# Last attention head: TensorE's steps in a fixed order between half sums of the output projection

## The chip, the cores and the metric

The kernel runs on one core of a Trainium2 chip. The metric is the device time of one execution in microseconds, from the first to the last instruction and what lies around them; the median of several runs stands for a kernel. TensorE's clock is 2.4 GHz, or 1.2 GHz where it is throttled.

## The reference

The model is a trunk of two residual layers on a sequence of 1024 tokens of width 1024, in float32, with a norm at the end. The change lies in the first layer. It has two branches on one normed input: an SSD scan (Mamba-2, 1024 channels), and a differential attention with 8 heads. An attention head has two query and two key maps of width 64 and one value of width 128:

```python
s = einsum(q, k) * scale + bias[rel]          # two maps, causal
p = softmax(s)
w = p[:, :, 0] - lam * p[:, :, 1]
o = rmsnorm(einsum(w, v), subln_w) * (1 - lam_init)
y_b = o * silu(g)
h = x + concat([y_a, y_b]) @ w_out            # w_out: 2048 x 1024
```

The second layer (a gated linear recurrence) has the same kind of output projection, `out_proj`.

## The kernel before

Matmuls of the projections run in split float32: an operand is a high part and a rest, and a product is three matmuls (high by high, high by rest, rest by high). One group of 12 such matmuls of 512 columns (four blocks of 128 in the inner dimension, three products each) adds four input blocks of one token block into one PSUM bank. I call it a half sum: two of them (`kq` 0 and 1) make a sum over 8 blocks of 128, which is all of one branch.

**The attention of one head** is `att_core` (from line 592). A head has 8 query blocks of 128 tokens, block `i` sees `i + 1` key blocks. `soft(i)` issues the scores of both maps on TensorE (line 613, into the PSUM tag `big`, two buffers), on DVE the bias and the maximum (lines 617 and 621), on ACT the exponential with its sum (line 627), on DVE the reciprocals (631 to 633) and the weighted difference of the two maps (line 634). `values(i)` transposes the difference on TensorE (line 645, into `s1`), copies it to SBUF on ACT (line 647) and multiplies it with the values (line 649). In the trace such a matmul of 128 columns in plain float32 counts as two. After four blocks `norm` scales, squares and sums on ACT (657, 660), takes the power on GpSimd (line 150) and multiplies on DVE (663); a `tail` later transposes the result (668), gates it on DVE (695) and stores it to HBM (696). Block `i + 1`'s scores are traced ahead of block `i`'s transposes.

**The output projection** is `out_proj` (from line 716). Its early part reads the SSD branch: 16 tiles `u`, split on ACT and DVE (lines 709 and 710), weights in two column halves `n`, and for each half 16 half sums, whose sums DVE adds to the input rows (line 767). That is 32 half sums, 384 matmuls at line 187. The late part does the same with the attention's output, which it reads back from HBM (lines 706, 712, 713), and ends in the next layer's norm.

**What sets the order.** The framework's scheduler decides the order of each engine's instructions from a time model. Code under `manual_schedule(engines={PE})` is the exception: there TensorE's instructions stand in the order in which the code issues them. Before the change only the SSD branch stood under it (line 902). `layer0` traces the heads one after the other, then `out_proj`, and the scheduler puts the early half sums into the heads' gaps where their inputs are there. The inputs come when the last projection that reads the layer's normed input is over: the projection of head 7 (line 176), which the scheduler puts beside head 5. So heads 6 and 7 have the early half sums beside them: the 16 of the first column half beside the first six blocks of head 6, the 16 of the second half from there on through head 7.

Of the kernel before, what the change touches and what calls it, by code (L numbers as in the profile page):

```python
# [70 lines left out]
def run(pieces):  # L71
    for _ in pieces:
        pass
# [515 lines left out]
    out += [(qs[m], (ks[m], xs[m])) for m in range(2)]  # L589


def att_core(S, h, qk, V, sg, yb, tail):

    nc = S.nc
    hh = h % 2
    near = S.t("ph" if h % 2 else "cm", [P, 256])

    for i in range(8):
        o = 127 - 16 * i
        nc.sync.dma_start(near[16 * i:16 * i + 16],  # L600
                          S.tz_d[h, o:o + 16 * 383].rearrange("(p w) -> p w", w=383)[:, 0:256])
    def soft(i):
        n = (i + 1) * P
        isl = slice(i * P, i * P + P)
        pp, zz = [], []
        for m in range(2):
            s = S.ps("big")
            f = max(n - 256, 0)
            for k0 in range(0, n, 512):
                kn = min(512, n - k0)  # L610
                q, ks = qk[m]
                for j in range(2):
                    nc.tensor.matmul(s[:, k0:k0 + kn], lhsT=q[:, isl], rhs=ks[j][:, k0:k0 + kn],  # L613
                                     start=(j == 0), stop=(j == 1))
            mx = S.sm.tile([P, 1], F32, name="mx")
            p = S.t(f"p{m}", [P, L])
            nc.vector.tensor_tensor_reduce(p[:, f:n], s[:, f:n], near[:, 256 - (n - f):], 1.0, -3.0e38,
                                           op0=ALU.add, op1=ALU.max, accum_out=mx)
            if f:
                mf = S.sm.tile([P, 1], F32, name="mf")  # L620
                nc.vector.tensor_tensor_reduce(p[:, :f], s[:, :f], bc(S.far[:, h:h + 1], [P, f]), 1.0, -3.0e38,  # L621
                                               op0=ALU.add, op1=ALU.max, accum_out=mf)
                nc.vector.tensor_scalar(mx, mx, mf, -1.0, op0=ALU.max, op1=ALU.mult)  # L623
            else:
                nc.vector.tensor_scalar(mx, mx, -1.0, None, op0=ALU.mult)
            z = S.sm.tile([P, 1], F32, name=f"z{m}")
            nc.scalar.activation(p[:, :n], p[:, :n], AF.Exp, bias=mx, accum_out=z)  # L627
            pp.append(p)
            zz.append(z)
        r = S.sm.tile([P, 2], F32, name="rr", bufs=8)  # L630
        nc.vector.reciprocal(r[:, 0:1], zz[1])
        nc.vector.scalar_tensor_tensor(r[:, 0:1], r[:, 0:1], zz[0], S.nlam, op0=ALU.mult, op1=ALU.mult)
        nc.vector.reciprocal(r[:, 1:2], zz[0])
        nc.vector.scalar_tensor_tensor(pp[0][:, :n], pp[1][:, :n], r[:, 0:1], pp[0][:, :n],
                                       op0=ALU.mult, op1=ALU.add)
        return pp[0], r[:, 1:2]

    def values(i, w, iz, po):
        n = (i + 1) * P
        wT = S.t("wT", [P, L])  # L640
        for k0 in range(0, n, 512):
            kn = min(512, n - k0)
            pt = S.ps("s1")
            for j in range(kn // P):
                nc.tensor.transpose(out=pt[:, j * P:j * P + P],  # L645
                                    in_=w[:, k0 + j * P:k0 + j * P + P], identity=S.ident)
            nc.scalar.copy(wT[:, k0:k0 + kn], pt[:, :kn])  # L647
        for j in range(i + 1):
            nc.tensor.matmul(po[:, i % 4, :], lhsT=wT[:, j * P:j * P + P], rhs=V(j, hh),  # L649
                             start=(j == 0), stop=(j == i))  # L650
        zis.append(iz)

    def norm(q, po):
        o = S.t("o", [P, 4, P])
        so = S.sm.tile([P, 4], F32, name="so")
        for iq in range(4):
            nc.scalar.activation(o[:, iq], po[:, iq], AF.Copy, scale=zis[iq])
        for iq in range(4):
            jk = S.t("junk", [P, P])
            nc.scalar.activation(jk, o[:, iq], AF.Square, accum_out=so[:, iq:iq + 1])  # L660
        ro = S.sm.tile([P, 4], F32, name="ro")
        S.rstd(ro, so, 1.0 / P, EPS)
        nc.vector.tensor_tensor(o, o, bc(ro.unsqueeze(2), [P, 4, P]), op=ALU.mult)

        def tail():
            pt = S.ps("s1")
            for iq in range(4):
                nc.tensor.transpose(out=pt[:, iq * P:iq * P + P], in_=o[:, iq], identity=S.ident)
            sl = slice(q * 512, q * 512 + 512)
            emit_y(S, pt, S.subw, sg[:, sl], yb[:, sl])  # L670

        return tail

    zis = []
    po = None
    w = soft(0)
    for i in range(8):
        nxt = soft(i + 1) if i < 7 else None
        if i % 4 == 0:
            po = S.ps("s1", [P, 4, P])  # L680
        values(i, *w, po)
        w = nxt
        if i % 4 == 1 and tail is not None:
            tail()
        if i % 4 == 3:
            tail = norm(i // 4, po)
            zis = []
    return tail


def emit_y(S, pt, wcol, gate, dst):
# [26 lines left out]
def out_proj(S, y_d, wcols, x_d, x1_tags, rs_a, finish):  # L718
# [12 lines left out]
    def sums(ws, ys):  # L731

        for t in range(0, NT, 2):
            pas = [S.ps("pj") for _ in range(2)]
            order = ((0, 0), (1, 0), (0, 1), (1, 1)) if t in (0, NT - 2) else ((0, 0), (0, 1), (1, 0), (1, 1))
            for j, kq in order:
                hf, tt = divmod(t + j, 4)
                y = ys[hf][4 * kq:4 * kq + 4]
                S.mm_tm(pas[j], ws[kq], *([z[:, i, tt * P:tt * P + P] for z in y] for i in range(2)),
                        first=kq == 0, last=kq == 1)  # L740
                if t == NT - 2 and j == 1:
                    S._wprep(S.wpos + kq)
                if kq == 1:
                    yield hf, tt, pas[j]

    y = [[], []]
    for hf in range(2):
        for k in range(0, KT, 2):
            y[hf] += load(hf, k, "u", "u")
        if hf == 0:  # L750
            ws = pair()
# [3 lines left out]
    late = [[], []]  # L755
    for n in range(2):
        if n:
            ws = pair()
        for hf, t, pa in sums(ws, y):
            if t % 2 == 0:  # L760
                x1 = x1s[hf, n, t // 2] = S.t(next(tags), [P, 2, 512])
                r0 = hf * 512 + t * P
                nc.sync.dma_start(x1, x_d[r0:r0 + 256, n * 512:n * 512 + 512].rearrange("(t p) n -> p t n", p=P))
            if rs_a is None:
                nc.vector.tensor_tensor(x1[:, t % 2], pa, x1[:, t % 2], op=ALU.add)
            else:
                nc.vector.scalar_tensor_tensor(x1[:, t % 2], pa, rs_a[:, hf * 4 + t:hf * 4 + t + 1], x1[:, t % 2],
                                               op0=ALU.mult, op1=ALU.add)
            if n == 1 and t % 2 == 1:
                k = 4 * hf + t - 1  # L770
                late[0] += load(0, KT + k, *(("A", "A") if k < 6 else ("u", "u")))
    tags1 = "V", "V", "G", "G", "p0", "p0", "p1", "wT"
    ss = [S.sm.tile([P, 4, 2], F32, name="ss4", bufs=2) for _ in range(2)]
    for n in range(2):
        ws = pair()
        rss = []
        for hf, t, pa in sums(ws, late):
            if n == 0 and hf == 0:
                for k in (2 * t, 2 * t + 1):
                    late[1] += load(1, KT + k, tags1[k])  # L780
            xr = x1s[hf, n, t // 2][:, t % 2]
            nc.vector.tensor_tensor(xr, pa, xr, op=ALU.add)
            jk = S.t("ey", [P, 512])
            nc.scalar.activation(jk, xr, AF.Square, accum_out=ss[hf][:, t, n:n + 1])
            if n == 0:
                finish.early(xr)
                continue
            sr = S.sm.tile([P, 1], F32, name="sr")
            nc.vector.tensor_tensor(sr, ss[hf][:, t, 0:1], ss[hf][:, t, 1:2], op=ALU.add)
            rs = S.sm.tile([P, 1], F32, name="rs")  # L790
            S.rstd(rs, sr, 1.0 / D, EPS)
            rss.append(rs)
            finish.row(hf, t, [x1s[hf, m, t // 2][:, t % 2] for m in range(2)], rs)
            if t == 3:
                finish(hf, x1s, rss)
                rss = []
# [93 lines left out]
def layer0(S, x, x1_d, u1):  # L890
# [34 lines left out]
    for h in range(8):  # L925
# [8 lines left out]
                sg = S.proj_gate(u, ("G", "bt" if h == 4 else "G"))  # L934
        elif h < 7:
            Vn = S.proj_v(u)
        tail = att_core(S, h, qk, V, sg[h % 2], yb[h], tail)
    tail()
    out_proj(S, lambda k, n: (ya if k < 8 else yb)[k % 8:k % 8 + n], S.ssdw, x,
             ["V", "V", "bt"] + ["A"] * 5, rsa,  # L940
             next_norm(S, u1, x1_d, S.norm_c[:, 8:16]))


def layer1(S, x1_d, u, out):
# [62 lines left out]
        pass  # L1007

    finish.early, finish.row = early, row
    out_proj(S, lambda k, n: yo[k:k + n], None, x1_d, ["V", "V"] + ["A"] * 5 + ["bt"], None, finish)  # L1010


def hgrn_core(S, hd, g1, f, K, V, g2, att, lvm, dgm, yo):
# [184 lines left out]
```

## Time and profile before

| | |
|---|---|
| median of 3 runs | 2192.46 us (2192.11 to 2192.67) |
| the profiled execution | 2190.09 us |
| its span, first to last instruction | 2188.2 us |
| busy share of the span: TensorE, DVE, ACT, GpSimd | 98%, 57%, 38%, 10% |
| mean granted TensorE clock | 0.999 |

The busy time of TensorE's matmuls is modelled to their ends and they are pipelined, so the durations of neighbours overlap: the distance of their starts is what one costs. Idle time is counted where an engine has no instruction, and is put down to what ended it. All times below are in microseconds from the start of the span.

### The profile page before, as it was taken

Reading aid. Unit: us, or ns where it says so; the run is one execution under the profiler, and the core shown is the slowest. Engines: PE = TensorE matmul, PEld = TensorE weight load, DVE = VectorE, ACT = ScalarE, POOL = GpSimd, SP = SyncE. Lnnn points to the kernel's source line nnn. Section 1 sums busy time; section 2 is a strip of 40 time slices with the busy share of each in tenths; the row PEclk is TensorE's granted clock in tenths of the full one; section 3 lists DMA queues with packets and bytes.
Section 4 is the critical chain, followed back from the end, with each engine's and each line's share of the span. In section 5 each row is a group of like instructions: output and inputs, shape, how many; then the busy total and the mean of one; then the engine's idle time right before and its main releaser. Section 6 shows DMA issues by size and latency. Waiting matters only on the chain.

```text
span 2188.2 us, 37614 instructions
## 1 busy us (share of the span) xinstructions
PE 2149.8 (98%) x15332; PEld 1827.5 (84%) x15332; DVE 1248.3 (57%) x2816; ACT 826.0 (38%) x1863; POOL 211.9 (10%) x216
## 2 busy tenths in 40 slices
PE   7999999999999999999999999999999999999998
PEld 5788888898898987877888888898989898988886
DVE  4766877565556557654344555555555555557423
ACT  4444444354445446443332233223332332234213
POOL 1021221100000000000010100101010101011000
PEclk9999999999999999999999999999999999999999
DMA  4322222322212225223221111111111111125412
GB/s 141 77 71 74 77 75 76 88 66 54 59 49 65 59 56 163 87 66 126 82 64 55 45 41 47 49 50 49 49 49 49 49 49 49 49 67 171 130 39 96
DMA packets 146752, 156.32 MB, mean 71 GB/s; under 512 B 9567, under 2 KB 113409, under 8 KB 146580
## 3 DMA queue, kind: packets, MB, share of 16 engines
q1 hardware_dynamic: 141124, 139.84, 21.4%
q0 software_dynamic: 3280, 9.90, 2.1%
q10 hardware_dynamic: 2176, 4.19, 0.5%
q8 instruction: 120, 1.97, 0.4%
q14 instruction: 52, 0.43, 0.1%
HBM read 120.08 MB, written 25.43 MB: 66 GB/s over the span
## 4 chain that ended last, share of the span: by engine, by line
PE 93%; DVE 2%; DMA 2%; ACT 2%; issue 1%; SPq 0%; POOL 0%; POOLq 0%; ACTq 0%; DVEq 0%
PE pj L176 48%; PE pj L187 26%; PE big L613 3%; PE s L649 3%; PE big L1054 2%; PE s L645 1%; PE big L1142 1%; PE big L1144 1%; PE s L1131 1%; PE big L525 1%; PE big L1096 1%; PE s L1158 1%; PE s L161 1%; PE big L519 1%; DMA A<-in_x 1%
## 5 line engine op out<-in xcount | busy, mean ns | idle before, releaser
L176 PE MATMUL pj<-u,w_hi 128*128 128x512 f32 x3072 | 980.9, 397 | 1.9 <-ACT u L163 1.2
L176 PEld LDWEIGHTS pj<-u,w_hi 128*128 128x128 f32 x3072 | 567.3, 188 | 120.8 <-issue 2.6
L176 PE MATMUL pj<-u,w_lo 128*128 128x512 f32 x1536 | 603.0, 393 | 0.0
L187 PE MATMUL pj<-w_hi,u 128*128 128x256 f32 (+1 forms) x2112 | 480.2, 316 | 2.5 <-DVE A L244 1.0
L187 PEld LDWEIGHTS pj<-w_hi,u 128*128 128x128 f32 x2112 | 350.4, 190 | 27.3 <-DVE A L244 1.4
L176 PEld LDWEIGHTS pj<-u,w_lo 128*128 128x128 f32 x1536 | 288.9, 188 | 59.9 <-issue 0.2
L187 PE MATMUL pj<-w_lo,u 128*128 128x256 f32 (+1 forms) x1056 | 331.5, 314 | 1.3 <-DVE w_lo L135 1.3
L135 DVE TENSOR_TENSOR w_lo<-w_raw,w_hi 128x1024 fp32r<-128x1024 f32 x152 | 186.0, 1244 | 136.2 <-ACT w_hi L134 136.0
L187 PEld LDWEIGHTS pj<-w_lo,u 128*128 128x128 f32 x1056 | 201.0, 190 | 13.3 <-DVE w_lo L135 2.2
L134 ACT CAST w_hi<-w_raw 128x1024 fp32r<-128x1024 f32 x152 | 152.5, 1047 | 156.8 <-PE pj L176 102.0
L243 ACT ACTIVATE th<-pj 128x512 f32<-128x512 f32 x96 | 57.2, 596 | 204.4 <-PE pj L176 204.1
L244 DVE SCALAR_TENSOR_TENSOR A<-th,pj 128x512 f32<-128x512 f32 x80 | 55.1, 688 | 136.0 <-ACT th L243 135.4
L627 ACT ACTIVATE p<-p,mx 128x256 f32<-128x256 f32 (+7 forms) x128 | 98.5, 771 | 67.8 <-DVE mx L623 60.7
L150 POOL TENSOR_TENSOR ro<-rs_t,mhalf 128x4 f32<-128x4 f32 x48 | 53.5, 1114 | 671.2 <-DVE rs_t L149 523.4
L976 POOL TENSOR_SCALAR A<-th,fN,fB 128x512 f32<-128x512 f32 x32 | 49.0, 1532 | 472.4 <-ACT th L973 464.7
L613 PE MATMUL big<-A 128*128 128x512 f32 (+3 forms) x384 | 90.0, 354 | 2.4 <-DVE mf L621 1.8
L647 ACT COPY wT<-s 128x512 f32<-128x512 f32 (+2 forms) x96 | 45.9, 478 | 96.9 <-PE s L645 96.1
L649 PE MATMUL s<-V,wT 128*128 128x128 f32 x576 | 79.6, 275 | 2.2 <-ACT wT L647 2.2
L649 PEld LDWEIGHTS s<-V,wT 128*128 128x128 f32 x576 | 75.1, 191 | 6.3 <-ACT wT L647 3.1
L1038 DVE TENSOR_TENSOR A<-A,p 128x512 f32<-128x512 f32 x96 | 65.8, 685 | 23.5 <-PE big L1054 23.0
L446 DVE SCALAR_TENSOR_TENSOR A<-V,convw,A 128x1023 f32<-128x1023 f32 (+2 forms) x48 | 61.1, 1276 | 31.7 <-ACT A L438 31.5
L1033 DVE TENSOR_TENSOR p<-p,p 128x512 f32<-128x512 f32 x96 | 66.1, 689 | 15.6 <-PE big L1090 6.5
(305 smaller groups left out, 2751.4 us busy)
## 6 DMA issues: line engine op xcount, KB each, us to landing
w_raw<-in_even_w_in SPq DMA_DIRECT2D x32, 512.0 KB, 5.4
w_raw<-in_odd_w_in SPq DMA_DIRECT2D x64, 256.0 KB, 3.6
w_raw<-in_odd_w_in SPq DMA_DIRECT2D x32, 512.0 KB, 4.2
w_raw<-in_even_w_in SPq DMA_DIRECT2D x48, 256.0 KB, 4.0
A<-A POOLq DMA_DIRECT2D x32, 256.0 KB, 5.5
w_raw<-in_even_w_out SPq DMA_DIRECT2D x16, 512.0 KB, 4.8
yo<-ey SPq DMA_DIRECT2D x32, 256.0 KB, 2.0
w_raw<-in_odd_w_out SPq DMA_DIRECT2D x16, 512.0 KB, 4.9
```

Source lines behind the costliest of these rows:

```text
L134: nc.scalar.copy(hq, raw)
L135: nc.vector.tensor_tensor(lq, raw, hq.bitcast(F32), op=ALU.subtract)
L176: nc.tensor.matmul(out, lhsT=ww[:, k, ms], rhs=uu[k][:, sl], start=(n == 0), stop=(n == 3 * KT - 1))
L187: nc.tensor.matmul(out, lhsT=uu[k], rhs=ww[:, k, :], start=(first and k == 0 and j == 0), stop=(last and k == kt - 1 and j == 2))
L243: nc.scalar.activation(th, pj, AF.Tanh, scale=0.5)
L244: nc.vector.scalar_tensor_tensor(out, view(th), 1.0, view(pj), op0=ALU.add, op1=ALU.mult)
L446: nc.vector.scalar_tensor_tensor(cv[:, d:], rp[:, :L - d], S.convw[:, k, ci:ci + 1], cv[:, d:], op0=ALU.mult, op1=ALU.add)
L613: nc.tensor.matmul(s[:, k0:k0 + kn], lhsT=q[:, isl], rhs=ks[j][:, k0:k0 + kn], start=(j == 0), stop=(j == 1))
L627: nc.scalar.activation(p[:, :n], p[:, :n], AF.Exp, bias=mx, accum_out=z)
L649: nc.tensor.matmul(po[:, i % 4, :], lhsT=wT[:, j * P:j * P + P], rhs=V(j, hh), start=(j == 0), stop=(j == i))
L1033: nc.vector.tensor_tensor(q, q, bc(t0, [P, L // (2 * h), h]), op=ALU.mult)
L1038: nc.vector.tensor_tensor(k, k, bc(halves(Ts[h], 1)[1], [P, L // (2 * h), h]), op=ALU.mult)
```

## The change

`att_core` becomes a generator. It yields twice after `soft(0)`, once after each group of transposes with its copy (one group for blocks 0 to 3, two for blocks 4 to 7), and once at the end of each block: 22 yields in all. `out_proj` becomes a generator that yields after every early half sum, whether or not it completes a sum. Heads 0 to 6 are run through at once, as before. For head 7 `layer0` opens a block with a fixed order for TensorE, goes through the head step by step with one half sum after each, adds two more half sums and the last tail, and leaves the block; the 8 half sums left and the late part follow. The second layer's call runs its generator through.

```diff
-def att_core(S, h, qk, V, sg, yb, tail):
+def att_core(S, h, qk, V, sg, yb, tail, out):
...
             nc.scalar.copy(wT[:, k0:k0 + kn], pt[:, :kn])
+            yield
...
     w = soft(0)
+    yield
+    yield
     for i in range(8):
...
-        values(i, *w, po)
+        yield from values(i, *w, po)
...
+        yield
-    return tail
+    out.append(tail)
...
-                if kq == 1:
-                    yield hf, tt, pas[j]
+                yield (hf, tt, pas[j]) if kq == 1 else None
...
-        for hf, t, pa in sums(ws, y):
+        for z in sums(ws, y):
+            yield
+            if z is None:
+                continue
+            hf, t, pa = z
...
-        tail = att_core(S, h, qk, V, sg[h % 2], yb[h], tail)
-    tail()
-    out_proj(S, lambda k, n: (ya if k < 8 else yb)[k % 8:k % 8 + n], S.ssdw, x,
-             ["V", "V", "bt"] + ["A"] * 5, rsa,
-             next_norm(S, u1, x1_d, S.norm_c[:, 8:16]))
+        tails = []
+        core = att_core(S, h, qk, V, sg[h % 2], yb[h], tail, tails)
+        if h < 7:
+            run(core)
+            tail = tails[0]
+
+    op = out_proj(S, lambda k, n: (ya if k < 8 else yb)[k % 8:k % 8 + n], S.ssdw, x,
+                  ["V", "V", "bt"] + ["A"] * 5, rsa,
+                  next_norm(S, u1, x1_d, S.norm_c[:, 8:16]))
+    with S.tc.manual_schedule(engines={mybir.EngineType.PE}):
+        for _ in core:
+            next(op)
+        for _ in range(2):
+            next(op)
+        tails[0]()
+    run(op)
```

How the order moves. TensorE in head 6, from the values of its block 0 to the scores of block 3, before (`big` are scores, `s` with `ident` are transposes, `s` with `V` are values, `pj` are half sums; 18 more matmuls of half sums follow the last row):

```order
L649 MATMUL s_7903<-V,wT 128x128
L613 MATMUL big<-A 128x512 x2
L187 MATMUL pj<-w_hi,u 128x512
L187 MATMUL pj<-w_lo,u 128x512
L187 MATMUL pj<-w_hi,u 128x512 x2
L187 MATMUL pj<-w_lo,u 128x512
L645 MATMUL s_7937<-ident,p_7884 128x128 x2
L187 MATMUL pj<-w_hi,u 128x512
L613 MATMUL big<-A 128x512 x2
```

The same place now, on to the transposes of block 2:

```order
L650 MATMUL s_7903<-V,wT 128x128
L613 MATMUL big<-A 128x512 x2
L645 MATMUL s_7937<-ident,p_7884 128x128 x2
L613 MATMUL big<-A 128x512 x2
L650 MATMUL s_7903<-V,wT 128x128 x2
L613 MATMUL big<-A 128x512 x2
L613 MATMUL big<-A 128x128 x2
L669 MATMUL s_7943<-ident,o 128x128 x4
L645 MATMUL s_7979<-ident,p_7913 128x128 x3
```

No half sum is left in head 6 up to the transposes of its block 6. Before, 204 matmuls of half sums stood between its first scores and that place. TensorE where the first half sum stands now, behind the values of head 6's block 5 and the first scores of head 7 (23 matmuls of half sums begin with the last row):

```order
L645 MATMUL s_8133<-ident,p_8054 128x128 x2
L650 MATMUL s_8079<-V,wT 128x128 x6
L669 MATMUL s_8143<-ident,o 128x128 x4
L613 MATMUL big<-A 128x128 x4
L187 MATMUL pj<-w_hi,u 128x512
```

From there on two half sums stand with each of head 7's blocks 0 to 3 and three with each of blocks 4 to 7. Before, head 7 had this on TensorE at its blocks 3 and 4, where no half sum stands from the values of block 2 to those of block 5:

```order
L649 MATMUL s_8432<-V,wT 128x128 x4
L613 MATMUL big<-A 128x512 x2
L613 MATMUL big<-A 128x384 x2
L645 MATMUL s_8610<-ident,p_8522 128x128 x4
L645 MATMUL s_8616<-ident,p_8522 128x128
L613 MATMUL big<-A 128x512 x2
L613 MATMUL big<-A 128x384 x2
L649 MATMUL s_8608<-V,wT 128x128 x5
```

ACT at the exponentials of head 6's block 1 (the rows at line 627), behind the splits of the SSD branch's tiles `u`, before:

```order
L709 ACTIVATE u<-u,cols 128x512 x4
L647 COPY wT<-s_7547 128x512
L709 ACTIVATE u<-u,cols 128x512 x3
L579 ACTIVATE A<-pj 64x512
L709 ACTIVATE u<-u,cols 128x512 x3
L647 COPY wT<-s_7553 128x512
L627 ACTIVATE p_7884,z_7887<-p_7884,mx 128x256
L627 ACTIVATE p_7893,z_7896<-p_7893,mx 128x256
```

and now:

```order
L713 ACTIVATE u<-u,cols 128x512 x2
L647 COPY wT<-s_7547 128x512
L713 ACTIVATE u<-u,cols 128x512 x5
L579 ACTIVATE A<-pj 64x512
L713 ACTIVATE u<-u,cols 128x512
L647 COPY wT<-s_7553 128x512
L713 ACTIVATE u<-u,cols 128x512 x2
L627 ACTIVATE p_7884,z_7887<-p_7884,mx 128x256
L627 ACTIVATE p_7893,z_7896<-p_7893,mx 128x256
```

The two copies of head 5's last block move ahead of some splits; the exponentials stay behind the last of them.

## Rows read from the trace of the kernel before

**Rows 1.** The page's first part: busy time, share of the span, instructions of each engine.
```profile
PE 2149.8 (98%) x15332; PEld 1827.5 (84%) x15332; DVE 1248.3 (57%) x2816; ACT 826.0 (38%) x1863; POOL 211.9 (10%) x216
```
**Rows 2.** Busy time by stretches: length, PE, PEld, DVE, ACT, POOL, PEclk, DMA, GB/s.
```profile
856.20:870.00 13.80, 10.36 (x55) 7.75 (x54) 12.82 (x27) 13.70 (x26) 1.03 (x2) 1.00 1.09 318
870.00:927.70 57.70, 57.62 (x300) 49.01 (x301) 35.49 (x110) 25.66 (x67) 3.14 (x4) 1.00 0.32 97
927.70:1036.40 108.70, 102.92 (x535) 85.56 (x533) 55.30 (x150) 42.65 (x111) 3.69 (x4) 1.00 0.29 93
```
**Rows 3.** TensorE's groups from 856.2 to 927.6: busy, mean ns, idle before.
```profile
L187 PE MATMUL pj<-w_hi,u 128*128 128x512 f32 x136 | 44.3, 397 | 0.8 <-DVE u L710 0.8
L187 PE MATMUL pj<-w_lo,u 128*128 128x512 f32 x68 | 26.8, 394 | 0.8 <-DVE w_lo L135 0.8
```
**Rows 4.** TensorE in order of time: start, duration, instruction, idle time before it.
```profile
927.69 0.60 PE L645 MATMUL s<-ident,p 128*128 128x128 f32 x4
...
1002.13 0.48 PE L187 MATMUL pj<-w_hi,A 128*128 128x512 f32 x1
1002.44 0.40 PE L187 MATMUL pj<-w_lo,A 128*128 128x512 f32 x1
1002.67 0.62 PE L187 MATMUL pj<-w_hi,A 128*128 128x512 f32 x2
...
1005.40 0.62 PE L187 MATMUL pj<-w_hi,A 128*128 128x512 f32 x2
```
**Rows 5.** ACT in order of time, at head 6's block 1.
```profile
867.47 1.95 ACT L709 ACTIVATE u<-u,cols 128x512 fp32r<-128x512 f32 x3
...
869.92 0.51 ACT L627 ACTIVATE p<-p,mx 128x256 f32<-128x256 f32 x1
...
870.42 0.50 ACT L627 ACTIVATE p<-p,mx 128x256 f32<-128x256 f32 x1
```
**Rows 6.** DVE in order of time, at the same block.
```profile
873.88 0.75 DVE L767 SCALAR_TENSOR_TENSOR V<-pj,rsa,V 128x512 f32<-128x512 f32 x1 [0.95 <-DMA V<-in_x]
...
874.80 0.48 DVE L634 SCALAR_TENSOR_TENSOR p<-p,rr,p 128x256 f32<-128x256 f32 x1
```
**Rows 7.** DVE in order of time, head 7, blocks 4 and 5, without half sums.
```profile
972.36 0.88 DVE L634 SCALAR_TENSOR_TENSOR p<-p,rr,p 128x640 f32<-128x640 f32 x1
...
973.74 0.68 DVE L621 CUSTOM_DVE_ANT_0 p<-big,far 128x512 f32<-128x512 f32 x1
...
974.69 0.82 DVE L621 CUSTOM_DVE_ANT_0 p<-big,far 128x640 f32<-128x640 f32 x1
...
976.78 0.16 DVE L631 RECIPROCAL rr<-z 128x1 f32<-128x1 f32 x1 [0.75 <-ACT p L627]
...
977.21 0.69 DVE L663 TENSOR_TENSOR o<-o,ro 128x512 f32<-128x512 f32 x1
977.82 1.01 DVE L634 SCALAR_TENSOR_TENSOR p<-p,rr,p 128x768 f32<-128x768 f32 x1
```
**Rows 8.** ACT in order of time, two exponentials of head 7.
```profile
970.97 0.81 ACT L627 ACTIVATE p<-p,mx 128x640 f32<-128x640 f32 x1
...
971.78 0.92 ACT L627 ACTIVATE p<-p,mx 128x768 f32<-128x768 f32 x1
```
**Rows 9.** TensorE in order of time, at the start and the end of the span.
```profile
18.46 1.22 PE L176 MATMUL pj<-u,w_hi 128*128 128x512 f32 x2 [0.90 <-ACT u L163]
...
21.19 0.63 PE L176 MATMUL pj<-u,w_hi 128*128 128x512 f32 x1
...
23.73 0.39 PE L176 MATMUL pj<-u,w_hi 128*128 128x512 f32 x1
...
2179.76 0.39 PE L187 MATMUL pj<-w_hi,wT 128*128 128x512 f32 x1
```
**Rows 10.** Busy time by stretches, after the last matmul.
```profile
2184.00:2186.00 2.00, 0.00 (x0) 0.00 (x0) 0.09 (x1) 0.06 (x1) 0.00 (x0) 0.50 0.52 211
```
**Rows 11.** DVE's groups from 872.0 to 919.9, with the idle time before them.
```profile
L617 DVE CUSTOM_DVE_ANT_0 p<-big,cm 128x256 f32<-128x256 f32 x12 | 5.1, 423 | 10.6 <-PE s L645 8.9 <-PE big L613 1.7
```

More of the change, by code (lines that the diff above doesn't have):

```diff
@@ L776, in out_proj @@
         rss = []
-        for hf, t, pa in sums(ws, late):
+        for z in sums(ws, late):
+            if z is None:
+                continue
+            hf, t, pa = z
             if n == 0 and hf == 0:
@@ L1009, in layer1 @@
     finish.early, finish.row = early, row
-    out_proj(S, lambda k, n: yo[k:k + n], None, x1_d, ["V", "V"] + ["A"] * 5 + ["bt"], None, finish)
+    run(out_proj(S, lambda k, n: yo[k:k + n], None, x1_d, ["V", "V"] + ["A"] * 5 + ["bt"], None, finish))
 def hgrn_core(S, hd, g1, f, K, V, g2, att, lvm, dgm, yo):
```

## The prediction

> **What bounds the kernel now.** I read the page's first part first: TensorE is busy for 98% of the span [rows 1]. A TensorE idle for even a microsecond is therefore time on the clock, and any edit that only reorders TensorE is judged by one thing: how much idle time it makes or removes. Then the busy time by stretches, for the place that the change touches: heads 6 and 7 of the attention and the output projection beside them [rows 2]. From 856.2 us, where the first half sum of the projection starts, to 1036.4 us, TensorE is idle for 3.4 us in the first stretch, 0.1 us in the second and 5.8 us in the third: 9.3 us together. That is all that better filling could ever win here.
>
> What keeps it so full is seen in the groups of TensorE's instructions up to 927.6 us [rows 3]: 136 and 68 matmuls of the projection, 204 or 17 half sums, stand between head 6's steps. TensorE has something to do while DVE and ACT work on a softmax block. A half sum costs 2.73 us: 12 matmuls lie between the rows at 1002.67 and at 1005.40 [rows 4]. So 204 are worth 46.4 us.
>
> **The change, part by part.**
>
> *The yields, the extra argument, the generator's wrapping.* They issue nothing; each engine executes the same set of instructions. Zero.
>
> *Head 6 loses its filler.* This is the main term. By the order excerpts all 17 half sums that stood within head 6 now stand behind its last scores: the projection is traced inside the fixed block, together with head 7. The projection of head 7, which fills head 5 and the beginning of head 6, is unchanged, so up to 856.2 us the two programs are alike. From there to the first half sum TensorE has only head 6's own scores, transposes and values, and waits for DVE and ACT. When does that first half sum come?
>
> - Start. ACT has the exponentials of block 1 behind the last of the 16 splits of the SSD branch's tiles, in both orders. Before, ACT goes from one to the next without idling, and the second exponential (from 870.42, 0.50 us) ends at about 871 [rows 5]. I take the same time. The weighted difference (I call it combine) of block 1 starts at 874.80, behind 0.95 us of idling for an input row and 0.75 us of evacuating a sum [rows 6]. Both are gone: it starts at 873.1 and ends at 873.6.
> - Steps. Head 7 has a stretch without half sums already, and I read the pace there [rows 7]. From combine of block 4 (972.36) to that of block 5 (977.82) it takes 5.46 us: combine, the second map's maximum of block 5, the first map's of block 6, then a wait for ACT's exponential, the reciprocals, and 0.69 us of normalising the output (only in some steps). Plain, that is 4.8 us at 768 columns. The next block's maximum follows combine at once (its second part is at 973.74): the loop goes through DVE and ACT, and TensorE isn't in it. Per 128 columns combine changes by 0.13 (0.88 to 1.01), each of the two maxima by 0.14 (0.68 to 0.82) and the exponential by 0.11 (0.81 to 0.92, [rows 8]): 0.5 us. So blocks 2 to 6 take 3.2, 3.8, 4.3, 4.8 and 5.3 us, 21.4 together; with two normalisings and one gated output (0.69, 0.69, 0.75) 23.5.
> - End. The half sums wait behind head 7's first scores, which need the PSUM that block 7's two maxima (1.35 us each, estimated from the same slope) free: 2.7, and 0.4 for the scores.
>
> Together 873.6 + 23.5 + 2.7 + 0.4 = 900.2 us. At that point TensorE stands where it stood at 927.69 before [rows 4], but the 204 half-sum matmuls are still to come: 900.2 + 46.4 - 927.7 = **+18.9 us**. Bounds: if no exponential is ever waited for (0.75 us per step in rows 7, five steps) the start is 896.5; if every step takes 5.46 us it is 904.9. I take 900.2, since the measured step has the same instructions in the same order.
>
> *Head 7 in the fixed order.* It had the second column half's half sums, in runs that left its blocks 3 and 4 with none; the idle time after 927.7 is 5.8 us [rows 2]. Now each step gets two or three half sums (5.5 or 8.2 us), against 4 to 5.3 us of pace. Covered: I expect 1.5 us where the transposes of blocks 6 and 7 of head 6 follow each other with their ACT copies, and 1.5 us in the late part, whose loads of the attention's output now have 8 more half sums ahead of them. 3.0 instead of 5.8: **-2.8 us**. Bounds: 0 and 7. The half sums form 7 more separate runs than before; a switch costs about 0.08 us (0.31 instead of 0.23 between 1002.13 and 1002.44, [rows 4]), two a run: **+1.1 us**.
>
> *The queues.* On SP's queue the weights of the projection's second half go out earlier among the other transfers, behind the output of head 6's last tail and one load; they are needed some 50 us after that. The last tail's store and the loads behind it keep their order and get more time. ACT and DVE have no instruction more. Zero, covered by the half sums; without that cover a late weight costs what it does in this trace, under 1 us.
>
> *TensorE's clock.* The program begins with slow matmuls: the dense ones start at 18.46, 512 columns take 0.63 us at 21.19 and 0.39 at 23.73 [rows 9], so the slow time is between 2.7 and 5.3 us, some 4. And at the end the granted clock stands at 0.50 of full (1.2 GHz) within some 4 us of the last matmul, at 2179.76 [rows 9, 10]. Between 859 and 864 us TensorE will have nothing to do, because block 1 waits behind ACT's splits, so I expect the clock to fall there once. While the loop goes through DVE and ACT a slower TensorE costs nothing; the rise, at the start of head 7, costs half of some 4 us: **+2.0 us**. Bounds: 0 if it never falls; 8 if TensorE's own work in the stretch, doubled, becomes the loop (first rival).
> The Trainium skill, page "TensorE: Matmul & The Clock Gate", section "Part 1: The HAM clock gate (the 'warmup' mystery)", says that half rate is the default and that only sustained activity lifts it. By that rule the clock would stay low through the whole sparse stretch, not only at its ends; no run here shows a stretch like that yet.
>
> **Sum.** 18.9 - 2.8 + 1.1 + 2.0 = +19.2 us. The profiled execution took 2190.09 us, so 2209.3; the median of the runs is 2.4 us above it, which gives **2212 us**.
>
> **Rivals.**
>
> 1. *TensorE at 1.2 GHz becomes the loop of head 6.* For: it is nearly 70% idle there. Its own work between 856.2 and 927.7 is 71.5 - 46.4 - 3.5 = 21.6 us with full clock, some 18 of it after 870; doubled that is 36 us, against 30 of the loop: +6, 2218 us. Against: with that load it is no longer idle, so the clock would rise again. The page named above would have this one. Chance 0.20.
> 2. *The fixed order stalls head 7.* Blocks 1 to 3 have two half sums to hide two maxima, two exponentials and combine; if the transposes come round too early, some 2 us per step for three steps, +6: 2218 us. For: nothing else may pass a waiting instruction. Against: pace 3.2 to 4.3 us under 5.5 of cover. Chance 0.13.
> 3. *Not slower: without half sums in TensorE's queue head 6 runs away.* Before, DVE's maxima waited 10.6 us for TensorE, whose scores were queued behind half sums [rows 11], so part of head 6's length was TensorE's queue, and a free TensorE lets DVE run on. I have counted that: it is why 900.2 stands there and not 927.7. To come out even the first half sum would have to start by about 881, that is five steps and the end in 7 us, where the one step measured takes 4 even without its wait and its normalising. And had the scheduler moved half sums into the gap in spite of the fixed block, the order would show them. Chance 0.05.
>
> **How the numbers follow.** My forecast has 0.62, the rivals 0.20, 0.13 and 0.05. A measurement of this kernel can tell about 0.2%, 4.4 us, from no change. Low end: start at 896.5 (-3.7), no idle time left later (-3.0), no fall of the clock (-2.0): +10.5, 2203 us. High end: start at 904.9 (+4.7), one of the two slower rivals and part of the other (+10): +34, 2226 us. Slower by over 0.2% is everything but the third rival and a far tail: 0.95; within 0.2%: 0.03; faster: 0.02.
>
> **What would show it.** In the profile after: half sums first at about 900 us and none before; TensorE idle for about 25 us or more between 856 and 900, ended mostly by combine and by the maxima; DVE no longer waiting for scores there; DVE's steps of head 6 3 to 5.5 us apart; hardly a wait of TensorE in head 7; the granted clock under 1.00 somewhere between 859 and 905. I am wrong if half sums start by 885, if TensorE's idle time over 856 to 1056 stays near 10 us, or if head 7 has waits of microseconds in each step.

## The result and the profile after

| | before | after |
|---|---|---|
| median of 6 runs, us | 2192.57 (2191.53 to 2194.26) | **2206.85** (2205.28 to 2207.39) |
| profiled execution, us | 2190.09 | 2207.39 |
| its span, us | 2188.2 | 2205.5 |
| mean granted clock | 0.999 | 0.995 |

The ratio is 1.0061, 95% interval 1.0051 to 1.0071: slower by 0.6%. The forecast was 2212 us, 2203 to 2226. From profile to profile it forecast +19.2 us, and +17.3 came; between the medians it is +14.3.

Of the 17.3, 1.7 came ahead of the place that the change touches. In this one execution TensorE's clock fell in a dense stretch of head 5, and the projection of head 7, which ends just ahead of head 6's steps, ended at 857.97 instead of 856.25. The same matmuls before, and then after (columns as in [rows 2]):

```profile
844.00:848.00 4.00, 4.00 (x19) 3.27 (x19) 2.46 (x8) 2.38 (x4) 0.00 (x0) 1.00 0.17 66
844.00:848.00 4.00, 4.00 (x13) 3.15 (x12) 2.47 (x8) 2.37 (x4) 0.00 (x0) 0.63 0.17 66
```

The two runs below that add matmuls and double the maxima have the same matmuls there and end this projection at 856.04 and 856.93. So I take the 1.7 us for scatter between executions, and count head 6 from the end of the projection. Why the clock fell there stays open.

The page's first part hardly shows it, against [rows 1]: TensorE is busy 6.5 us longer and idle 10.8 us longer in a span of 17.3 us more.

```profile
PE 2156.3 (98%) x15332; PEld 1832.6 (83%) x15332; DVE 1250.2 (57%) x2816; ACT 826.3 (37%) x1863; POOL 212.0 (10%) x216
```

Busy time by stretches after (columns as in [rows 2]) shows the place: TensorE is idle for 6.0 and 8.5 us in the first two, and the seventh number (granted clock) is under 1.00 in the same two.

```profile
856.20:870.00 13.80, 7.78 (x43) 6.85 (x43) 13.23 (x32) 13.18 (x25) 1.03 (x2) 0.75 1.04 337
870.00:900.00 30.00, 21.51 (x117) 16.91 (x117) 25.08 (x91) 18.51 (x58) 3.14 (x4) 0.89 0.49 126
900.00:927.70 27.70, 25.75 (x143) 21.99 (x144) 14.04 (x51) 12.18 (x36) 1.04 (x1) 1.00 0.18 60
927.70:960.00 32.30, 32.30 (x169) 27.33 (x169) 16.94 (x62) 13.23 (x35) 1.01 (x1) 1.00 0.01 5
960.00:1000.00 40.00, 38.45 (x202) 32.39 (x201) 23.72 (x42) 17.35 (x36) 1.64 (x2) 1.00 0.50 163
1000.00:1055.00 55.00, 54.87 (x242) 45.05 (x241) 14.02 (x17) 9.69 (x18) 0.00 (x0) 1.00 0.23 78
```

TensorE in order of time after. The first gap, 5.07 us, is a wait for ACT's copy of head 5's last block, which stands behind ACT's splits of the tiles `u`, as block 1's exponentials do; then shorter gaps follow, ended by the combine (line 634), the copies and the maxima (621). The first half sum starts at 901.42, where 900.2 was forecast. The last row is the transposes at which TensorE stood at 927.69 before [rows 4], now with 23 half-sum matmuls ahead of them.

```profile
859.25 0.48 PE L613 MATMUL big<-A 128*128 128x256 f32 x2
864.80 1.11 PE L645 MATMUL s<-ident,p 128*128 128x128 f32 x4 [5.07 <-ACT wT L647]
...
893.70 0.66 PE L645 MATMUL s<-ident,p 128*128 128x128 f32 x4 [1.27 <-DVE p L634]
895.12 1.16 PE L613 MATMUL big<-A 128*128 128x512 f32 x4 [0.76 <-DVE mf L621]
...
899.36 0.44 PE L613 MATMUL big<-A 128*128 128x128 f32 x2 [1.09 <-DVE mf L621]
...
901.42 0.45 PE L187 MATMUL pj<-w_hi,u 128*128 128x512 f32 x1
...
906.70 0.60 PE L645 MATMUL s<-ident,p 128*128 128x128 f32 x4
```

DVE after, the combines of head 6's blocks 1 to 6: 3.8, 4.7, 4.4, 5.5 and 4.3 us apart. These answer to the one step of [rows 7], and show again a wait for an exponential, a gated output (699) and a normalised one (664).

```profile
874.24 0.48 DVE L634 SCALAR_TENSOR_TENSOR p<-p,rr,p 128x256 f32<-128x256 f32 x1
...
878.06 0.62 DVE L634 SCALAR_TENSOR_TENSOR p<-p,rr,p 128x384 f32<-128x384 f32 x1
...
879.65 0.75 DVE L699 SCALAR_TENSOR_TENSOR ey<-s,subw,bt 128x512 f32<-128x512 f32 x1 [0.40 <-PE s L669]
...
882.78 0.75 DVE L634 SCALAR_TENSOR_TENSOR p<-p,rr,p 128x512 f32<-128x512 f32 x1
...
886.71 0.16 DVE L631 RECIPROCAL rr<-z 128x1 f32<-128x1 f32 x1 [0.92 <-ACT p L627]
...
887.17 0.89 DVE L634 SCALAR_TENSOR_TENSOR p<-p,rr,p 128x640 f32<-128x640 f32 x1
...
892.03 0.69 DVE L664 TENSOR_TENSOR o<-o,ro 128x512 f32<-128x512 f32 x1
892.64 1.01 DVE L634 SCALAR_TENSOR_TENSOR p<-p,rr,p 128x768 f32<-128x768 f32 x1
...
896.94 1.15 DVE L634 SCALAR_TENSOR_TENSOR p<-p,rr,p 128x896 f32<-128x896 f32 x1
```

The granted clock in steps of 4 us after (the number behind POOL's): it falls to 1.2 GHz while TensorE has nothing from 859.7 to 864.8, is back at 2.4 GHz for part of the stretch from 868 to 872, falls again while TensorE waits 2.12 us for a copy up to 873.24, and is at 2.4 GHz from 880 on, though TensorE is still idle for a fifth of the time and more and no half sum has come yet.

```profile
860.00:864.00 4.00, 0.00 (x0) 0.00 (x0) 3.77 (x8) 4.00 (x7) 0.52 (x1) 0.76 1.04 394
864.00:868.00 4.00, 3.20 (x14) 3.20 (x15) 3.94 (x10) 3.98 (x8) 0.51 (x1) 0.50 1.10 309
868.00:872.00 4.00, 2.17 (x12) 1.42 (x11) 3.97 (x9) 3.95 (x10) 0.00 (x0) 0.89 1.18 232
872.00:876.00 4.00, 2.51 (x7) 1.59 (x8) 3.68 (x18) 3.56 (x17) 0.07 (x1) 0.54 0.68 225
876.00:880.00 4.00, 3.62 (x14) 3.00 (x14) 3.21 (x14) 1.41 (x4) 0.97 (x1) 0.61 0.01 4
880.00:884.00 4.00, 3.14 (x20) 2.68 (x21) 3.62 (x14) 2.06 (x5) 0.00 (x0) 1.00 0.58 178
884.00:888.00 4.00, 2.93 (x19) 2.24 (x17) 3.01 (x14) 2.83 (x7) 0.00 (x0) 1.00 0.06 21
```

### The profile page after: what moved, and what is told of

It reads as the page before. It is cut to its first block, busy times and chain, and to the rows that moved or that the text cites. A ratio compares the mean times of both kernels' runs of the same rounds, so it can differ in the third digit from the quotient of the medians.

```text
span 2205.5 us, 37624 instructions
## 1 busy us (share of the span) xinstructions
PE 2156.3 (98%) x15332; PEld 1832.6 (83%) x15332; DVE 1250.2 (57%) x2816; ACT 826.3 (37%) x1863; POOL 212.0 (10%) x216
## 4 chain that ended last, share of the span: by engine, by line
PE 93%; DMA 2%; ACT 2%; DVE 2%; issue 1%; SPq 0%; POOL 0%; POOLq 0%; ACTq 0%; DVEq 0%
PE pj L176 48%; PE pj L187 26%; PE big L613 3%; PE s L650 2%; PE big L1075 2%; PE s L645 1%; PE big L1163 1%; PE big L1165 1%; PE s L1152 1%; PE big L525 1%; PE big L1117 1%; PE s L1179 1%; PE s L161 1%; PE big L519 1%; PE big L522 1%
## 5 line engine op out<-in xcount | busy, mean ns | idle before, releaser
L613 PEld LDWEIGHTS big<-A 128*128 128x128 f32 x384 | 66.6, 193 | 15.5 <-DVE mf L621 3.7
L1059 DVE TENSOR_TENSOR A<-A,p 128x512 f32<-128x512 f32 x96 | 65.9, 686 | 23.5 <-PE big L1075 23.0
```

The source lines that it names most:

```text
L1059: nc.vector.tensor_tensor(k, k, bc(halves(Ts[h], 1)[1], [P, L // (2 * h), h]), op=ALU.mult)
```

## The experiments

Each kernel ran beside the kernel before on the same chip; the ratios are to that. The kernel before had medians of 2193.1 to 2193.5 in these rounds.

**The fixed block taken away, the trace order kept** (e1_free_order).

```diff
-    with S.tc.manual_schedule(engines={mybir.EngineType.PE}):
-        for _ in core:
+    for _ in core:
...
```

> The changed kernel without the block that fixes TensorE's order; head 7 and the projection are still traced step by step in turn. Theory (the fixed block alone keeps the half sums out of head 6, and their absence is the whole loss): half sums start at about 856 us again, TensorE idles about 9 us between 856 and 1036, and the time is that of the kernel before, 2190 to 2195 us. Rival (the new trace order, the later loads or the wrapping cost something by themselves): half sums start early but the time stays above 2198 us.

Measured: 2192.58 us, ratio 0.9997 (0.9988 to 1.0007). The first half sum starts at 857.05. The block alone makes the loss; generator, queues and trace order make none that can be measured. This run frees head 7's order as well as head 6's, so by itself it does not say where the block costs; the runs further down, which keep a fixed order in head 7 and give head 6 its half sums back, do. The next runs ask what paces head 6 without them.

**Twice the far maxima on DVE, in the changed kernel and in the one before** (e4_after_double_max, e5_before_double_max; the same edit).

```diff
                                                op0=ALU.add, op1=ALU.max, accum_out=mf)
+                if h == 6:
+                    nc.vector.tensor_tensor_reduce(p[:, :f], s[:, :f], bc(S.far[:, h:h + 1], [P, f]), 1.0, -3.0e38,
+                                                   op0=ALU.add, op1=ALU.max, accum_out=mf)
```

> The changed kernel with the far part of each maximum of head 6 (blocks 2 to 7, both maps) done twice on DVE; the second pass writes the same values. Twelve passes of 0.28 to 0.95 us, 7.4 us together. Theory (head 6 goes at the pace of DVE and ACT): all but the two passes that fit into DVE's waits for ACT (block 5's and block 6's first map, 0.69 and 0.75 us) lie on the path, so the first half sum starts about 6 us later, at 907.4 (906.4 to 909), and the time rises by as much, to 2211.5 to 2214.5. Rival (TensorE or ACT paces the head, DVE has slack): the start and the time move by under 2 us.

> The kernel before with the same doubled passes on DVE in head 6, 7.4 us together. Theory (there the half sums cover the softmax, and DVE waited 10.6 us for scores): the time moves by under 1.5 us, 2191 to 2194. Rival (head 6's softmax was on the path before, too): 4 to 7 us more, 2196 to 2200.

Measured: 2213.14 us in the changed kernel (ratio 1.0092, 1.0077 to 1.0107), 6.3 us above its 2206.85. In the kernel before 2192.34 (0.9996, 0.9987 to 1.0006): nothing. The same work on DVE is free under the half sums and lies on the path without them. The expected start was off: in the first of the two the half sums start at 911.50, not 907.4, because the scheduler now put the transposes and values of head 6's block 6 ahead of them. The combines do not show a plain delay by the added passes either. Counted from the end of the projection, block 5's comes 3.45 us later than in the changed kernel (895.05 less 856.93, against 892.64 less 857.97), with 4.7 us of passes added ahead of it, and block 6's 7.6 us later. Between these two, block 7's first maxima now stand ahead of block 6's combine (2.3 us), DVE waits 1.81 us for TensorE, and the clock is at 0.70 to 0.72 from 892 to 900. So it is partly chance that 6.3 us came where 6 were expected. That work added to DVE costs time here, and none in the kernel before, does not hang on this. DVE and TensorE in order of time in that kernel:

```profile
895.05 1.02 DVE L637 SCALAR_TENSOR_TENSOR p<-p,rr,p 128x768 f32<-128x768 f32 x1
...
902.29 0.75 DVE L702 SCALAR_TENSOR_TENSOR ey<-s,subw,G 128x512 f32<-128x512 f32 x1 [1.81 <-PE s L672]
...
903.52 1.15 DVE L637 SCALAR_TENSOR_TENSOR p<-p,rr,p 128x896 f32<-128x896 f32 x1
```
```profile
904.82 1.09 PE L648 MATMUL s<-ident,p 128*128 128x128 f32 x4 [2.40 <-DVE p L637]
...
911.50 0.44 PE L187 MATMUL pj<-w_hi,u 128*128 128x512 f32 x1
```

**More matmuls to keep the clock up** (e3_dummy_clock).

```diff
             ws = pair()
+    if rs_a is not None:
+        for hf in range(2):
+            for z in y[hf]:
+                pj = S.ps("pj")
+                for j in range(4):
+                    nc.tensor.matmul(pj, lhsT=z[:, 0, 0:P], rhs=z[:, 0], start=True, stop=True)
+        yield
...
+    next(op)
     with S.tc.manual_schedule(engines={mybir.EngineType.PE}):
```

> The changed kernel with 64 more matmuls of 512 columns (four for each of the 16 tiles u, into a PSUM tile that nobody reads; about 14.7 us of TensorE) in head 6's blocks 0 to 3, where the granted clock fell to 0.50. Theory (a loop of DVE and ACT paces head 6, and TensorE at half clock is off it): the granted clock stays at 1.00 or near it between 860 and 880, the first half sum still starts at 901.4 us, give or take 1, and the time stays within 2 us of the changed kernel's 2206.9. Rival (the low clock is part of the loss): the first half sum starts 2 to 6 us earlier, at 895 to 899, and the time falls to 2201 to 2205.

Measured: 2208.27 us (ratio 1.0068, 1.0053 to 1.0083; 4 runs, 2204.51 to 2210.04). The stretches now have the clock at 1.00, and the first half sum starts at 901.40 against 901.42:

```profile
856.20:870.00 13.80, 12.86 (x66) 9.06 (x65) 12.81 (x28) 13.21 (x25) 1.03 (x2) 1.00 1.07 315
870.00:900.00 30.00, 24.85 (x151) 20.79 (x150) 23.64 (x91) 18.31 (x58) 3.14 (x4) 1.00 0.43 113
```
```profile
901.40 0.45 PE L187 MATMUL pj<-w_hi,u 128*128 128x512 f32 x1
```

The rival's gain came neither in the start nor in the time. That the start is the same to 0.02 us is chance, though. This execution ends the projection 1.9 us earlier (856.04), has block 6's transposes ahead of the first half sum, and loses time to the added matmuls: from 870 to 901 DVE waits 3.3 us for TensorE, where it waited 0.4. The stretch in which the two clocks differ tells more. It is over by block 3's combine:

```profile
880.79 0.75 DVE L634 SCALAR_TENSOR_TENSOR p<-p,rr,p 128x512 f32<-128x512 f32 x1
```

That is 24.75 us behind the end of the projection, against 24.81 in the changed kernel (882.78 less 857.97), with 0.6 us of waits for TensorE up to there. From these numbers I estimate that the half clock cost head 6 about 1 us at most, and the rival is out. Head 6's pace is DVE's and ACT's: in the changed kernel DVE is busy for 25.1 of the 30 us from 870 to 900 and waits for TensorE for 0.4.

**Half sums in head 6 and a fixed order in head 7** (e2_sixteen_ahead, e6_eighteen_ahead). The first:

```diff
+    for _ in range(16):
+        next(op)
     with S.tc.manual_schedule(engines={mybir.EngineType.PE}):
-        for _ in core:
-            next(op)
-        for _ in range(2):
-            next(op)
+        for i, _ in enumerate(core):
+            if i >= 10 or i in (3, 5, 7, 9):
+                next(op)
```

The second has 18 ahead and the steps `i in (3, 5, 7, 9) or 10 <= i < 21 and i != 12`.

> Sixteen half sums (the first column half) are traced ahead of head 7, outside the block with the fixed order, where the scheduler puts them into head 6 as before; the other 16 stand in the fixed block with head 7, one behind each of its blocks 0 to 3, three behind each of 4 to 7. Theory (the loss came from head 6's missing half sums, the fixed order as such costs nothing): half sums start at about 856 us, the only bare stretch is about 6 us of pace at head 6's last transposes and head 7's blocks 0 and 1, some 4 us idle, against 5.8 of idling that the order before had in head 7: 2190 to 2195 us. Rival (the fixed order costs in head 7): 2198 us or more.

> As the run with 16 ahead, but with 18 half sums ahead of the fixed block and 14 in it (one behind each of head 7's blocks 0 to 3, two or three behind each of 4 to 7), so that the scheduler has two for the place between head 6 and head 7. Theory: hardly any TensorE wait is left from 856 us to the late part, so 2 to 5 us less than the kernel before, 2187 to 2191 us. Rival (the idling comes back in another place, as late waits for a softmax or for the late part's loads): 2191 to 2195 us.

Measured: 2197.51 us (ratio 1.0020, 1.0011 to 1.0029) and 2197.71 (1.0018, 1.0009 to 1.0027). Both theories missed, and so did the rivals' numbers. Half sums do stand in head 6 again (from 856.12 and 856.59), and with them most of the loss is gone: about 4 us of 14 are left with the fixed order still in place in head 7. I put the 4 us down to where its half sums stand: at the ends of blocks 0 to 3, so that nothing lies between transposes and values, and TensorE waits for ACT's copy (4.7 us in four waits in the first of the two; it has 2.1 us more between head 6 and head 7, up to 926.89). The next runs test this. TensorE in the first of them, at head 7's blocks 0 and 2:

```profile
938.32 0.47 PE L187 MATMUL pj<-w_hi,u 128*128 128x512 f32 x1
938.64 0.39 PE L187 MATMUL pj<-w_lo,u 128*128 128x512 f32 x1
...
941.15 0.86 PE L613 MATMUL big<-A 128*128 128x384 f32 x4
...
950.04 0.93 PE L650 MATMUL s<-V,wT 128*128 128x128 f32 x6 [2.19 <-ACT wT L647]
950.73 0.67 PE L187 MATMUL pj<-w_hi,u 128*128 128x512 f32 x1
951.20 0.63 PE L187 MATMUL pj<-w_lo,u 128*128 128x512 f32 x1
...
955.16 1.48 PE L613 MATMUL big<-A 128*128 128x512 f32 x8
```

A half sum took 2.83 us (938.32 to 941.15), and 4.43 behind the wait of 2.19: the clock had fallen (0.72 from 952 to 956). So the wait of 2.19 us cost another 1.6 us in the dense work behind it. The kernel with 18 ahead waits for copies in the same way, and 3.47 us more at 992 for a sum that DVE had not yet added; the next runs take these one by one.

**The half sums behind the copies** (e7_behind_copies, e8_twenty_ahead). As the kernel with 18 ahead, with the steps `i in (1, 2, 4, 6, 8, 10, 11, 13, 14, 16, 17, 18, 19, 20)`; and 20 ahead with `i in (2, 4, 6, 8, 10, 11, 13, 14, 16, 17, 19, 20)`.

> As the run with 18 half sums ahead of the fixed block, but the 14 in the block stand elsewhere: one behind each of head 7's transposes with their copy (blocks 0 to 3 one, 4 to 7 two) and two more, where the earlier two kernels had those of blocks 0 to 3 at the block's end. Theory (the 4 us that those kernels lost came from waits of 0.5 to 2.2 us for ACT's copies in head 7's blocks 0 to 3, and from the half clock that followed): these waits fall to under 2 us together, the granted clock stays at 1.00 from 940 to 1000, and the time is 2188 to 2193 us. Rival (any fixed order in head 7 costs as much): 2196 us or more.

> 20 half sums ahead of the fixed block, 12 in it, one behind each group of head 7's transposes with its copy. Theory: two more half sums between head 6 and head 7, so the place at 931 to 940 us, where the kernel with 18 waited 2.5 us, is filled too; 2187 to 2192 us, and the waits of TensorE from 856 to 1000 us under 5 us. Rival (any fixed order in head 7 costs as much): 2196 us or more.

Measured: 2191.00 us (0.9991, 0.9982 to 0.9999) and 2195.58 (1.0012, 1.0003 to 1.0021). With 18 ahead the waits for copies from 940 to 984 are gone, as the theory had it, and so is the loss: the order in head 7 is still fixed, so it was the half sums missing from head 6 that cost the time. A new one is there: 3.0 us at 984, and 6.6 in the kernel with 20 ahead, which missed. TensorE, and then SP's waits, in the kernel with 18:

```profile
987.21 0.79 PE L187 MATMUL pj<-w_hi,u 128*128 128x512 f32 x1 [3.04 <-DVE A L774]
987.80 0.63 PE L187 MATMUL pj<-w_lo,u 128*128 128x512 f32 x1
```
```profile
SPq L710 <- PE big L613: 21.6, 1, 21.6
```

DVE cannot add the sum, because the load of its input row is issued only at 980.35: on SP's queue it stands behind a load of the late part, which waits 21.6 us for a buffer `A` that head 7's last scores free. In DVE's order two splits of the late part's inputs (line 717, with 2.0 us of waits for ACT) stand ahead of the sum, too; they came with the same loads, and the next run moves both together. Two PSUM buffers of `pj` hold what can't be drained, then TensorE stops.

**The late loads behind the last early half sum** (e9_late_loads_last on the last kernel with 18 ahead; e10_before_loads_last on the kernel before).

```diff
             if n == 1 and t % 2 == 1:
-                k = 4 * hf + t - 1
-                late[0] += load(0, KT + k, *(("A", "A") if k < 6 else ("u", "u")))
+                ks = (4 * hf + t - 1,) if rs_a is None else (0, 2, 4, 6) if hf and t == 3 else ()
+                for k in ks:
+                    late[0] += load(0, KT + k, *(("A", "A") if k < 6 else ("u", "u")))
```

> The kernel with 18 half sums ahead and 14 behind head 7's copies, and the loads of the late part's first eight inputs traced behind the last early half sum, so that the input rows of the last early sums no longer queue on SP behind a load that waits for head 7's last scores (21.6 us in the run without this). Theory (the 3.0 us wait at 984 us came from there): that wait goes, and with it the half clock after it (about 1.3 us): 2185 to 2190 us. Rival (the late loads, now later, are waited for at the start of the late part): as much is lost there, 2190 to 2195 us.

> The kernel before with the same later loads, no fixed order. Theory (the place without half sums in head 7's blocks 3 and 4, some 5 us of idling, came from the same queue): half sums stand there and the time falls by 2 to 5 us, to 2188 to 2191 us. Rival (the hole moves to another place, or the late part waits for its loads): within 1.5 us of the kernel before.

Measured: **2187.68 us**, ratio 0.9974 (0.9965 to 0.9983), for the first: faster than both kernels. All five input rows go out at 914.76, TensorE doesn't wait at 984 any more, and the clock stays at 1.00 from 960 to 1000. SP's queue and the stretch:

```profile
914.76 2.96 SPq L770 DMA_DIRECT2D A<-in_x  x5
```
```profile
960.00:1000.00 40.00, 39.33 (x218) 33.42 (x217) 27.12 (x65) 19.71 (x45) 1.62 (x2) 1.00 0.32 100
```

The second missed: 2200.43 us (1.0037, 1.0024 to 1.0049). Half sums did fill head 7's blocks 3 and 4 (38.5 us busy from 960 to 1000, 35.2 before), but then they were used up at about 988, and the late part, whose loads into `A` went out from 991 on, waited; TensorE's longest wait there is 4.9 us for the tile `G`, and from 1000 to 1055 it is idle for 8.1 us:

```profile
1000.00:1055.00 55.00, 46.88 (x214) 38.24 (x215) 17.94 (x34) 17.78 (x44) 1.64 (x2) 0.94 0.25 88
```

That is the rival's mechanism, the late part waiting for its loads, but not its number: it said within 1.5 us, and 7 came. Here later loads paid only where half sums were kept to cover them, as the fixed order does.

## Why the prediction was right, point by point

- **Head 6 loses its filler: +18.9 forecast, +18.4 measured**, counted from the end of the projection: (901.42 - 857.97) + 46.4 - (927.69 - 856.25). From the start of the span it is +20.1, with the 1.7 us that came before.
  - *Start:* the combine of block 1 ended at 874.7, not 873.6; ACT's second exponential came 1.0 us later (871.43 against 870.42 in [rows 5]), which belongs to that shift.
  - *Steps:* from the end of that combine to the end of block 6's (896.94 + 1.15) it took 23.4 us, forecast 23.5. Step by step, with the normalised and the gated outputs where they came, the first four were forecast as 3.9, 4.6, 4.3 and 5.5 and measured as 3.8, 4.7, 4.4 and 5.5: one measured step of head 7, scaled by columns, gave these within 0.2 us. The last was forecast as 5.3 and took 4.3, since block 7's first maxima stood behind block 6's combine. That the whole still fits within 0.1 us is luck: the forecast added a pace from start to start to the end of a combine, 0.7 us too little, and this made up for most of it.
  - *End:* the last maxima and scores took 3.3 us, forecast 3.1. Of that, 0.38 us is a wait for the transfer of head 7's swapped keys (`A<-A`). The upper bound of 904.9 does not follow: with five steps of 5.46 us the same sum gives 904.0.
  - The doubled maxima show that DVE's loop is on the path now and was not before.
- **Head 7: -2.8 forecast, -3.1 measured.** 2.7 us of idling are left after the first half sum (1.95, 0, 1.55 and 0.13 in the stretches above, less the 0.96 between 900 and 901.42), where 5.8 were [rows 2]. The sum fits better than its parts: 1.0 of the 1.5 us expected at head 6's last copies, 0.13 of the 1.5 expected in the late part, and 1.55 at 980, for the combine of head 7's last block, where none was expected. The second rival (2 us per step in head 7) is out for this order: two half sums per block, one of them between transposes and values, cover ACT's copy. The kernel with 16 ahead shows that it was near: without that one, the rival's 2.19 us wait appears.
- **Switches: +1.1.** 1.7 + 18.4 - 3.1 makes 17.0, the spans differ by 17.3, so 0.3 is left for this and all else; the term was too large.
- **Queues: 0.** It held: no wait of TensorE for a weight or an input row is left from 901.42 to 1055. The later runs show that this was close, too: with more half sums ahead of head 7's last scores the same queue costs 3.0 to 6.6 us.
- **The clock: +2.0 forecast, nothing of it paid where it was expected.** This is the term that failed. The forecast had one fall between 859 and 864, because block 1 waits, and a rise that costs at the start of head 7. The clock did fall there, in a wait for the copy of head 5's last block, rose, and fell once more; by the rows above it was at half for some 13.6 us up to 880. But it was back at 1.00 some 21 us before the first half sum, so no dense work behind it ran at 1.2 GHz, and head 6 itself lost about 1 us at most. The other cost of the clock in this execution, 1.7 us, lay in head 5, where the forecast had none. The first rival (TensorE as the loop, 2218 us) falls by the run with the clock kept at 1.00; its "nearly 70% idle" did not fit its own figures, 18 us of work in the 30 of the loop. By the rule of the Trainium skill, page "TensorE: Matmul & The Clock Gate", section "Part 1: The HAM clock gate (the 'warmup' mystery)", as the prediction read it, the clock would have stayed low through the whole sparse stretch: the trace agrees on the fall, and not on that reading, with 1.00 from 880 on and TensorE busy 3.14 and 2.93 of 4 us.
- **The median: +2.4 forecast.** The profiled execution of before lay 2.4 us under its median, and I gave the changed one the same; its own lies 0.5 above. Profile to profile the forecast missed by 1.9 us, in medians by 5.2: 2.9 of that is this correction (0.3 is rounding), which was scatter between executions and no property of the profile. The terms above are read from one execution of each kernel, so the sum of those that the change itself made, 15.6 us, is no surer than the 1 to 2 us by which executions differ; that the total came within 2 us is partly the 1.7 us from head 5.
- **The third rival** (not slower) is out by the start at 901.42, where about 881 was needed.
- **Signs that were wrong:** "TensorE idle for about 25 us or more between 856 and 900". It is 14.5 (6.0 + 8.5), since at half clock TensorE's own work takes longer and counts as busy: 28.0 us from the end of the projection to the first half sum, where the forecast had 21.6. With the clock at 1.00 the stretches show 6.1 us idle beside 14.7 of added matmuls, so 20.8. Nor were the waits "ended mostly by combine and by the maxima": of TensorE's waits from 856 to 901, 8.2 us ended with ACT's copies, 3.3 with the maxima, 2.5 with the combine. DVE's waits for scores did go: from 856 to 901 it waits for TensorE 0.4 us, where [rows 11] had 10.6.

## What to carry to other kernels

Filler is worth most where another engine's loop paces the work, so before an order is fixed, ask which stretch gives its filler away and how long that stretch runs at the other engines' pace: one step measured elsewhere in the trace, scaled by size, gave four of five steps here within 0.2 us. Check first that the two executions agree ahead of the change's place; here 1.7 of 17.3 us had come before it. A fixed order should put a piece of filler between the instruction that starts another engine's copy and the one that waits for it, and keep some for the loads that follow. A late load that waits for a buffer holds up what stands behind it on its queue, here for 21.6 us; look there before adding work in front.

## What was not expected of the hardware

- The granted clock came back to 1.00 in a stretch that was still a fifth to a quarter idle (880 to 888, 3.14 and 2.93 of 4 us busy).
- It also fell in dense work: to 0.63 from 844 to 848 in the profiled execution of the changed kernel, with TensorE busy for all 4 us, where the kernel before ran the same matmuls at 1.00. Four other kernels (e1_free_order, e7_behind_copies, e8_twenty_ahead, e9_late_loads_last) have 0.71 to 0.82 from 872 to 876, busy for all 4 us.
- A wait of TensorE of 2 to 3 us can cost more than its length where dense matmuls follow: behind 2.19 us a half sum took 4.43 instead of 2.83 us, and behind 3.04 us matmuls of 512 columns took 0.63 us, as against 0.39 at full clock. In head 6 of the changed kernel, where DVE and ACT set the pace, some 13.6 us with the clock low cost about 1 us at most.
